# A two-layer decoder trunk on one core: softmax placed behind its own scores, layer 1's memory attentions in one exponential phase, head transposes behind the next projection

## The chip, the cores and the metric

The kernel runs on one core of a Trainium2 chip. The metric is the time of one execution on the device in microseconds (us); less is better. The time of a kernel is the median of several runs. The core's engines work side by side, each through its own instructions in order: TensorE (PE, with its weight loads shown as PEld), VectorE (DVE), ScalarE (ACT), GpSimd (POOL) and SyncE (SP), which issues most DMAs. A semaphore wait at the head of an engine's queue holds everything behind it.

## The reference

512 tokens of width 1024 go through two layers. Layer 1 is a gated DeltaNet with 6 heads of 128, layer 2 a sliding-window attention with 12 heads of 64 and a sink per head. In both, four more heads of 64 attend to 256 fixed memory tokens. Each layer ends with an output projection and a gated feed-forward stage of width 2816.

```python
for layer in range(DEPTH):
    h = rms_norm(x, ln_mix[layer])
    mkv = mem_n @ w_mem_kv[layer]                       # memory keys and values
    if layer < N_A_LAYERS:
        mix_out, mem_q = gated_deltanet_mixer(h, ...)   # q, k, v = silu(conv(h @ w_in)), chunked scan
    else:
        proj = h @ swa_w_q[bl]
        q = apply_partial_rope(proj[..., :SWA_Q_W], cos, sin)
        mix_out = sliding_window_attention(q, shared_k, shared_v, swa_sinks[bl])
        mem_q = proj[..., SWA_Q_W:]
    mem_o = memory_attention(mem_q, mem_k, mem_v)       # softmax(q k / 8) v
    x = x + concatenate([mix_out, mem_o]) @ w_out[layer]
    x = x + swiglu(rms_norm(x, ln_ffn[layer]), w_gate_up[layer], w_down[layer])
return rms_norm(x, ln_final)
```

The softmax of the sliding window takes the sink into the maximum and into the denominator; that of the memories has neither sink nor mask.

## The kernel before

Activations lie transposed, features on the 128 partitions and the 512 tokens along a row. A matrix product in full precision is done as three products of parts (`mm3`, L206): each fp32 operand is split into a rounded high part and a remainder, so a projection of 128 output features is 8 × 3 matmuls of 128x512 into one PSUM bank (`pj`). Its weights come by a DMA (`wraw`, L187), are copied on ACT into the high part (`whi`, L148) and subtracted on DVE into the low part (`wlo`, L161); three pairs of these parts are kept, so weights are prepared ahead.

In layer 1 (`gdn`, L471) the order in the source is: key heads (projection, convolution of four taps as one ACT copy and three DVE steps, SiLU, four transposes on PE, L490 to L503); the decay matrices; gates; the inverses of 32x32 triangular blocks (`base_inverse`, L630: 31 pairs of small DVE steps on `big` and `btmp`, then DMAs); for each of two memory pairs an attention followed by three query heads; the solve of the triangular systems; value heads and the scan over 4 chunks of 128 tokens, for heads 0 to 2 and then 3 to 5 (`scan_step`, L695); the finish of the heads. In layer 2 (`swa`, L1077) a loop over six pairs of heads calls the projection and rotation of the next query pair, the scores of this pair, and `weigh` of the pair before, which holds softmax, transposes of the probabilities (`pt`, copied to `pf`) and the product with the values.

A scheduler of the framework gives each engine its order: the place in the source is a priority, and an instruction is put in line when what it reads is ready by the scheduler's own reckoning. On top of that, functions that need ACT's tables are kept together by hand: `use` (L130) puts a table load ahead, and `fn` (L140) binds each function to it; exponentials and logarithms need one table set, SiLU another. Each switch is an ACT_TABLE_LOAD. In layer 2 the transposes of a pair are bound behind the last score product given out before them.

PSUM has eight banks. Layer 1 uses three for `pj`, two for `g` (transposes, sums, half of the memories' scores) and three for `sc` (scan, other half of the scores, products with the values). Layer 2 uses two for `pj`, one for `g`, two for `qk` (one half of a pair's scores at a time), two for `pt` and one for `sc`. The scores of the window are masked and their maximum is taken by one DVE instruction per block (L752), which writes them to `sm` in SBUF and so frees the `qk` banks; the memories' exponentials in layer 1 read the PSUM banks directly (L142).

Of the kernel before, what the change touches and what calls it, by code (L numbers as in the profile page):

```python
# [18 lines left out]
P = 128  # L19
T = 512  # L20
D = 1024
KD = D // P
H = 6
NC = 4
# [4 lines left out]
EPS = 1e-6  # L29
# [6 lines left out]
LN_EXP = "natural_log_exp_and_others"  # L36
SILU_SIN = "silu_and_others"
# [51 lines left out]
class Builder:  # L89
# [381 lines left out]
    def gdn(self, gp):  # L471
        nc, a, tc = self.nc, self.a, self.tc
# [12 lines left out]
        kn, kg = [], []  # L485
# [22 lines left out]
        f = self.t(gp, [P, 3, NH], F32, "f")  # L508
# [10 lines left out]
        for h in range(H):  # L519
# [4 lines left out]
            ps = self.bank("g")  # L524
# [9 lines left out]
        qg = self.gcr  # L534
# [4 lines left out]
        z, mq, qm, q2 = [], [], [], []  # L539
# [7 lines left out]
        for m in range(2):  # L547
            mq.append(self.pair(self.mpool, f"mq{m}"))
            qm.append(self.t(self.mpool, [P, T], F32, f"qm{m}"))
            self.copy(qm[m], self.normed(4 * H + m))  # L550
        X, Tt = self.base_inverse(gp, base_in)
# [4 lines left out]
        def memory(m):  # L556
            self.use(LN_EXP)
            self.attention(gp, qm[m], self.memK[m], self.memV, m, mq[m])


        for h0 in (0, 3):
            memory(h0 // 3)
            ts = [self.conv_tile(h, self.t(gp, [P, T], F32, "qv", 5)) for h in range(h0, h0 + 3)]
            self.use(SILU_SIN)
            for h, t in zip(range(h0, h0 + 3), ts):
                self.fn(t, t, AF.Silu)
                ps = self.bank("g")
                for c in range(NC):
                    self.mm(ps[:, chunk(c)], kn[h][:, chunk(c)], t[:, chunk(c)])
                self.tt(nc.vector, DT[h], c4(ps), DT[h], ALU.mult)  # L570
                self.tt(nc.vector, qg[h], qg[h], c4(t), ALU.mult)
                sq = self.t(gp, [P, T], F32, "sq", 1)
                nc.scalar.activation(sq, t, AF.Square, scale=math.sqrt(EPS) * P)
                q2.append(self.t(self.dpool, [P, T], F32, f"q2{h}"))
                nc.sync.dma_start(q2[h], sq)
        AT = DT
        vt = []

        def values(heads):
            for h in heads:  # L580
# [8 lines left out]

        S = [None] * H  # L590

        def scan(heads):
            for c in range(NC):
# [127 lines left out]
        return new  # L721


    def attention(self, pool, q, kk, vv, m, out, sinks=None):
        self.weigh(pool, self.scores(pool, q, kk, sinks is not None), vv, m, out, sinks)

    def scores(self, pool, q, kk, win):

        nc = self.nc
        own = "pt" in self.pbufs  # L730
        half = [slice(0, 64), slice(64, P)]
        sm = [self.t(pool, [P, 2, 2, 2 * P], F32, "sm", 4 if own else 2) for _ in range(2)]
        sm = [t[:, n] for t in sm for n in range(2)]
        stats = self.t(pool, [P, 4, 2 * NC], F32, "stats", 2)
        mx, den, nm, es = (stats[:, i, :] for i in range(4))
        for n0 in range(0, NC, 2):
            if own:
# [23 lines left out]
                                accum_out=den[:, i:i + 1])  # L761
        return sm, mx, den, nm, es

    def weigh(self, pool, scores, vv, m, out, sinks):

        nc = self.nc
        win = sinks is not None
        own = "pt" in self.pbufs
        half = [slice(0, 64), slice(64, P)]
        sm, mx, den, nm, es = scores  # L770
        if win:
            sk = sinks.unsqueeze(2).to_broadcast([P, 2, NC])
# [10 lines left out]
                            accum_out=den[:, i:i + 1])  # L783
            self.tt(nc.vector, den, den, es, ALU.add)
        nc.vector.reciprocal(den, den)
        o = self.bank("sc")
        group = NC if own else 2
        for n in range(NC):
            if n % group == 0:
                pf = {}  # L790
            k0 = 1 if win and n == 0 else 0
            p = sm[n][:, :, k0 * P:]
            dn = den.rearrange("p (b n) -> p n b", b=2)[:, n, :]
            for b in range(2):
                if n % 2:
                    self.copy(p[:, b], p[:, b], scale=dn[:, b:b + 1])
                else:
                    self.ts(p[:, b], p[:, b], dn[:, b:b + 1], ALU.mult)
            pt = self.bank("pt" if own else "g", [P, 2, 2, P])
            for j in range(k0, 2):  # L800
                for b in range(2):
# [275 lines left out]
    def swa(self, sp):  # L1077
# [32 lines left out]
        def transpose_values():  # L1110
            v = vv.pop()
            pt = self.bank("g")
            for c in range(NC):
                self.tr(pt[:, c * P:(c + 1) * P], v[:, c * P:(c + 1) * P])
            vt = self.t(sp, [P, NC, P], F32, "vt")
            self.copy(vt.rearrange("p c i -> p (c i)"), pt)
            vv.extend(vt[:, c, :] for c in range(NC))

        def score(t):
            got[t] = self.scores(sp, qs[t], kk[0] if t < 6 else memK[t - 6], t < 6)  # L1120

        def weigh(t):
            mix[t] = self.pair(self.bpool)
            if t < 6:
                self.weigh(sp, got[t], vv, t, mix[t], sinks[:, t, :])
            else:
                self.weigh(sp, got[t], memV, t - 6, mix[t], None)

        got = {}
        queries(6)  # L1130
# [1 line left out]
        keys()  # L1132
        values()
        score(6)
        transpose_values()
        queries(0)
        score(7)
        weigh(6)
        last = 7
# [96 lines left out]
```

## Time and profile before

| | before |
|---|---|
| runs | 1160.89, 1162.48, 1162.56 us |
| median | 1162.48 us |
| profiled execution | 1162.59 us |
| span of its trace | 1160.8 us |
| granted TensorE clock | 0.998 |
| instructions | 19674 |
| PE idle in the span | 25.1 us |
| table loads (L133) | 13, 1.28 us each |

The profile shows one execution. The span is the time from the first to the last instruction; 1.8 us of the execution lie around it. A line of the timeline gives the start, the duration, engine, source line and operation, the tiles written and read, their shape, and in brackets how long the engine was idle before and what it waited for. Matmuls are pipelined, so the recorded time of one is longer than its share of PE's time. Layer 1's mixer ends at about 290 us; the feed-forward stages fill 335 to 655 and 831 to 1150 us; layer 2's attention is between 676 and 776 us.

### The profile page before, as it was taken

The numbers are of one execution on the slowest core, as the hardware profiler recorded it, in microseconds if no ns is written. First come the engines' busy times: TensorE is split into PE (matmuls) and PEld (weight loads), VectorE is DVE, ScalarE is ACT, GpSimd is POOL, SyncE is SP. The second block draws the span as 40 slices with busy tenths as digits, with TensorE's granted clock in tenths as the row PEclk, the third lists the DMA queues.
The fourth block names the chain that finished last, engine by engine and source line by source line (L and its number), as shares of the span: only waits on it lengthen the run. The fifth ranks groups of instructions, "written<-read, shape, count | busy, mean of one in ns | idle before, by whom it ended". The sixth has DMA issues, their size and how long they took to land.

```text
span 1160.8 us, 19674 instructions
## 1 busy us (share of the span) xinstructions
PE 1135.7 (98%) x7476; PEld 995.0 (86%) x7476; DVE 843.1 (73%) x1587; ACT 635.5 (55%) x1273; POOL 85.8 (7%) x97
## 2 busy tenths in 40 slices
PE   7999999999999999999999999999999999999996
PEld 6878777877899998899998777677899988999986
DVE  5754877767789987489866767758799843798754
ACT  7569563366556652256653547675566622566533
POOL 0210000000111100011100000010011100111000
PEclk9999999999999999999999999999999999999999
DMA  8433352225567744567723421143477743577232
GB/s 308 129 108 114 115 127 92 73 91 164 163 141 186 188 124 129 151 149 188 173 75 98 136 73 38 55 99 120 113 186 191 175 111 104 150 188 179 74 93 94
DMA packets 73971, 152.83 MB, mean 132 GB/s; under 512 B 17756, under 2 KB 18420, under 8 KB 73876
## 3 DMA queue, kind: packets, MB, share of 16 engines
q1 hardware_dynamic: 62356, 130.59, 35.9%
q0 software_dynamic: 11520, 20.98, 11.5%
q8 instruction: 59, 0.97, 0.4%
q14 instruction: 36, 0.29, 0.1%
HBM read 144.58 MB, written 6.96 MB: 131 GB/s over the span
## 4 chain that ended last, share of the span: by engine, by line
PE 86%; DVE 8%; ACT 2%; DMA 2%; issue 1%; SPq 0%; DVEq 0%; ACTq 0%
PE pj L154 40%; PE g L154 38%; PE sc L154 6%; DVE wlo L161 2%; PE pt L158 1%; DMA wraw<-in_wout 1%; PE g L158 1%; ACT sm L142 1%; DVE l L164 1%; ACT whi L148 1%; DMA wraw<-in_wmk 1%; DVE btmp L161 1%; DVE big L161 0%; DVE sm L752 0%; PE qk L154 0%
## 5 line engine op out<-in xcount | busy, mean ns | idle before, releaser
L148 ACT ACTIVATE whi<-wraw 128x512 fp32r<-128x512 f32 (+2 forms) x331 | 244.2, 745 | 271.9 <-PE pj L154 175.2
L161 DVE TENSOR_TENSOR wlo<-wraw,whi 128x512 fp32r<-128x512 f32 (+2 forms) x331 | 274.3, 838 | 108.6 <-ACT whi L148 102.7
L154 PE MATMUL pj<-h,whi 128*128 128x512 f32 (+1 forms) x676 | 266.4, 395 | 0.8 <-ACT h L148 0.5
L154 PE MATMUL pj<-l,whi 128*128 128x512 f32 (+1 forms) x676 | 265.2, 392 | 1.2 <-DVE l L164 1.2
L154 PE MATMUL pj<-h,wlo 128*128 128x512 f32 (+1 forms) x676 | 265.3, 393 | 0.0
L154 PE MATMUL g<-T,whi 128*128 128x256 f32 x1280 | 230.3, 282 | 0.0
L154 PEld LDWEIGHTS g<-T,whi 128*128 128x128 f32 x1280 | 197.6, 190 | 1.6 <-DVE fu L164 1.6
L154 PE MATMUL g<-T,wlo 128*128 128x256 f32 x640 | 180.1, 281 | 0.0
L154 PEld LDWEIGHTS pj<-h,whi 128*128 128x128 f32 x676 | 127.1, 188 | 29.7 <-issue 3.0
L154 PEld LDWEIGHTS pj<-l,whi 128*128 128x128 f32 x676 | 127.2, 188 | 28.4 <-DVE l L164 2.0
L154 PEld LDWEIGHTS pj<-h,wlo 128*128 128x128 f32 x676 | 127.3, 188 | 26.3 <-issue 1.9
L154 PE MATMUL g<-h,wlo 128*128 128x256 f32 (+1 forms) x508 | 146.2, 288 | 0.0
L154 PE MATMUL g<-l,whi 128*128 128x256 f32 (+1 forms) x508 | 146.1, 288 | 0.0
L154 PE MATMUL g<-h,whi 128*128 128x256 f32 (+1 forms) x508 | 146.0, 287 | 0.0
L154 PEld LDWEIGHTS g<-T,wlo 128*128 128x128 f32 x640 | 120.2, 188 | 0.0
L154 PEld LDWEIGHTS g<-l,whi 128*128 128x128 f32 x508 | 97.5, 192 | 1.2
L154 PEld LDWEIGHTS g<-h,whi 128*128 128x128 f32 x508 | 95.4, 188 | 1.2
L154 PEld LDWEIGHTS g<-h,wlo 128*128 128x128 f32 x508 | 95.4, 188 | 1.2 <-issue 0.2
L985 POOL DMA_DIRECT2D ws<-in_wgu x40 | 35.2, 879 | 722.9 <-ACT sq L151 246.2
L148 ACT ACTIVATE whi<-ws 128x512 fp32r<-128x512 f32 x80 | 50.4, 631 | 51.2 <-PE g L154 42.0
L161 DVE TENSOR_TENSOR fu<-pj,rstd 128x512 f32<-128x512 f32 (+1 forms) x34 | 22.4, 659 | 54.8 <-PE pj L154 54.8
L161 DVE TENSOR_TENSOR wlo<-ws,whi 128x512 fp32r<-128x512 f32 x80 | 54.8, 685 | 6.9 <-ACT whi L148 6.8
(345 smaller groups left out, 1633.0 us busy)
## 6 DMA issues: line engine op xcount, KB each, us to landing
wraw<-in_wgu SPq DMA_DIRECT2D x48, 512.0 KB, 4.1
ws<-in_wgu SPq DMA_DIRECT2D x80, 256.0 KB, 3.5
ws<-in_wgu POOLq DMA_DIRECT2D x80, 256.0 KB, 4.8
wraw<-in_wdn SPq DMA_DIRECT2D x48, 384.0 KB, 3.2
wraw<-in_win SPq DMA_DIRECT2D x26, 512.0 KB, 3.7
wraw<-in_wgu SPq DMA_DIRECT2D x40, 256.0 KB, 4.4
wraw<-in_wout SPq DMA_DIRECT2D x16, 512.0 KB, 3.6
wraw<-in_wdn SPq DMA_DIRECT2D x16, 256.0 KB, 2.7
```

Of the source, the lines that this page charges most:

```text
L142: ins = self.nc.scalar.activation(out, in_, func, **kw).ins
L148: self.copied = self.nc.scalar.activation(out, in_, AF.Copy, **kw).ins
L154: return self.nc.tensor.matmul(out, lhsT, rhs, start=start, stop=stop, skip_group_check=more).ins
L158: return self.nc.tensor.transpose(out, in_, self.ident[:k, :k]).ins
L161: return eng.tensor_tensor(out=out, in0=a, in1=b, op=op).ins
L164: self.nc.vector.scalar_tensor_tensor(out=out, in0=in0, scalar=scalar, in1=in1, op0=op0, op1=op1)
L985: nc.gpsimd.dma_start(s1, a22, accum_op=ALU.add)
```

## The change

Only the order of calls in the source changes; the same instructions are given out but for two table loads.

- Keys and values: the projection, convolution and SiLU of head h+1 are given out ahead of the transposes of head h.
- `attention` is taken apart into `scores`, `soften` (the softmax) and `weigh` (transposes and products).
- Memories of layer 1: scores and softmax of the first go ahead of the base inverses, those of the second between the second and third query's projection; all six SiLUs come behind in one phase. Two switches of tables go.
- Scan: the last chunk of the first three heads comes behind the values of the second three.
- Layer 2: softmax right behind the products of the pair before, an iteration's part earlier; six `sm` buffers instead of four, three of `stats` instead of two.

```diff
-        for h in range(H):
+        def key(h):
             k = self.conv_tile(H + h, self.t(gp, [P, T], F32, f"kn{h}"))
             self.fn(k, k, AF.Silu)
             kn.append(k)
+        key(0)
+        for h in range(H):
+            if h < H - 1:
+                key(h + 1)
+            k = kn[h]
             ps = self.bank("g")
...
+        def remember(m):
+            got = self.scores(gp, qm[m], self.memK[m], False)
+            self.soften(gp, got, None)
+            return got
+        self.use(LN_EXP)
+        got = remember(0)
         X, Tt = self.base_inverse(gp, base_in)
...
-        for h0 in (0, 3):
-            memory(h0 // 3)
-            ts = [self.conv_tile(h, self.t(gp, [P, T], F32, "qv", 5)) for h in range(h0, h0 + 3)]
-            self.use(SILU_SIN)
-            for h, t in zip(range(h0, h0 + 3), ts):
-                self.fn(t, t, AF.Silu)
...
+        ts = [query(0)]
+        self.weigh(gp, got, self.memV, 0, mq[0], False)
+        ts.append(query(1))
+        got = remember(1)
+        ts.append(query(2))
+        self.weigh(gp, got, self.memV, 1, mq[1], False)
+        self.use(SILU_SIN)
+        for h in range(H):
+            if h + 3 < H:
+                ts.append(query(h + 3))
+            t = ts[h]
+            self.fn(t, t, AF.Silu)
...
         def values(heads):
+            value(heads[0])
             for h in heads:
-                v = self.conv_tile(2 * H + h, self.t(gp, [P, T], F32, "qv", 5))
-                self.fn(v, v, AF.Silu)
+                if h + 1 in heads:
+                    value(h + 1)
+                v = vs[h]
...
         values(first)
-        scan(first)
+        scan(first, range(NC - 1))
         values(second)
+        scan(first, range(NC - 1, NC))
         self.use(LN_EXP)
         scan(second)
...
-        sm = [self.t(pool, [P, 2, 2, 2 * P], F32, "sm", 4 if own else 2) for _ in range(2)]
+        sm = [self.t(pool, [P, 2, 2, 2 * P], F32, "sm", 6 if own else 2) for _ in range(2)]
-        stats = self.t(pool, [P, 4, 2 * NC], F32, "stats", 2)
+        stats = self.t(pool, [P, 4, 2 * NC], F32, "stats", 3 if own else 2)
...
         for t in range(6):
             if t < 5:
                 queries(t + 1)
             score(t)
             weigh(last)
+            soften(t)
             last = t
         weigh(last)
```

What the scheduler makes of it, at three places. First PE at the transposes of key head 1, with the projection of the next key (`pj`) around them; before, and then after:

```order
L154 MATMUL pj_683<-h_479,wlo_680 128x512
L154 MATMUL pj_683<-h_484,whi_679 128x512
L154 MATMUL pj_683<-l_485,whi_679 128x512
L154 MATMUL pj_683<-h_484,wlo_680 128x512
L158 MATMUL g_661<-consts_66,kn_130_624 128x128 x4
L154 MATMUL pj_683<-h_489,whi_679 128x512
```

```order
L154 MATMUL pj_668<-h_484,wlo_665 128x512
L154 MATMUL pj_668<-h_489,whi_664 128x512
L154 MATMUL pj_668<-l_490,whi_664 128x512
L154 MATMUL pj_668<-h_489,wlo_665 128x512
L158 MATMUL g_698<-consts_66,kn_124_609 128x128 x4
L154 MATMUL pj_720<-h_454,whi_716 128x512
```

The transposes have moved behind the last three matmuls of that projection: 14 stood between them and those of key head 0, now 17.

Second ACT at the first memory of layer 1, behind its eight exponentials (`sm` from `g` and `sc`); `qv` is the first query:

```order
L142 ACTIVATE sm_1411,stats_1412<-sc_1428,stats_1412 128x256 x2
L133 ACT_TABLE_LOAD
L148 ACTIVATE sm_1410<-sm_1410,stats_1412 128x256 x2
L148 ACTIVATE sm_1411<-sm_1411,stats_1412 128x256
L148 ACTIVATE pf_1450<-g_1445 128x512
L148 ACTIVATE pf_1459<-g_1454 128x512
L148 ACTIVATE sm_1411<-sm_1411,stats_1412 128x256
L148 ACTIVATE qv_1497<-pj_1504,gains_67 128x512
```

```order
L142 ACTIVATE sm_1273,stats_1274<-sc_1290,stats_1274 128x256 x2
L148 ACTIVATE sm_1272<-sm_1272,stats_1274 128x256 x2
L148 ACTIVATE sm_1273<-sm_1273,stats_1274 128x256 x2
L148 ACTIVATE qv_1450<-pj_1457,gains_67 128x512
L148 ACTIVATE pf_1492<-g_1487 128x512
L148 ACTIVATE pf_1499<-g_1494 128x512
```

The table load is gone, and the fourth scaling and the copy of the query have moved ahead of the two `pf` copies.

Third DVE in an iteration of layer 2, at the reciprocal of the pair before; "ISA" rows at L752 (L774 after) are the masked maxima with the row that stores each one, `q` the next query's rotation, `wlo` a weight split. Before, all four maxima of the first half of scores stand ahead of the rows shown, and the last row is the first maximum of the second half; after, the first ISA row is the first maximum of the first half and the last one the second:

```order
L161 TENSOR_TENSOR stats_7305<-stats_7305 128x8
L161 TENSOR_TENSOR wlo_7925<-wraw_7922,whi_7924 128x1024
L785 RECIPROCAL stats_7305<-stats_7305 128x8
L168 TENSOR_SCALAR sm_7303<-sm_7303,stats_7305 128x128 x2
L168 TENSOR_SCALAR sm_7304<-sm_7304,stats_7305 128x256
L752 ISA sm_7429,stats_7430<-qk_7440,consts_66 128x256
```

```order
L161 TENSOR_TENSOR stats_7325<-stats_7325 128x8
L774 ISA sm_7448,stats_7450<-qk_7451,consts_66 128x128
L774 ISA stats_7450 128x1
L805 RECIPROCAL stats_7325<-stats_7325 128x8
L161 TENSOR_TENSOR q_7442<-q_7442,rs_7443 128x512
L168 TENSOR_SCALAR sm_7323<-sm_7323,stats_7325 128x128 x2
L168 TENSOR_SCALAR sm_7324<-sm_7324,stats_7325 128x256 x2
L774 ISA sm_7448,stats_7450<-qk_7451,consts_66 128x256
```

The reciprocal and the four scalings of the pair before have moved from behind the weight split to ahead of three of the four maxima of this pair's first half. On PE, 14 projection matmuls stood between the two halves of the same pair's scores, and now there are 18.

More of the change, by code (lines that the diff above doesn't have):

```diff
@@ L550, in gdn @@
             self.copy(qm[m], self.normed(4 * H + m))
+        query = lambda h: self.conv_tile(h, self.t(gp, [P, T], F32, "qv", 5))
+        def remember(m):
[4 more added lines that the diff above has]
+        got = remember(0)
         X, Tt = self.base_inverse(gp, base_in)
@@ L554, in gdn @@
             self.copy(kg[h][:, c, :], kg[h][:, c, :], scale=f[:, 2, i:i + 1])
-        def memory(m):
-            self.use(LN_EXP)
-            self.attention(gp, qm[m], self.memK[m], self.memV, m, mq[m])
-        for h0 in (0, 3):
-            memory(h0 // 3)
-            ts = [self.conv_tile(h, self.t(gp, [P, T], F32, "qv", 5)) for h in range(h0, h0 + 3)]
-            self.use(SILU_SIN)
-            for h, t in zip(range(h0, h0 + 3), ts):
-                self.fn(t, t, AF.Silu)
[L567 to L575, printed above, removed]
+        ts = [query(0)]
[10 more added lines that the diff above has]
+            self.fn(t, t, AF.Silu)
+            ps = self.bank("g")
+            for c in range(NC):
+                self.mm(ps[:, chunk(c)], kn[h][:, chunk(c)], t[:, chunk(c)])
+            self.tt(nc.vector, DT[h], c4(ps), DT[h], ALU.mult)
+            self.tt(nc.vector, qg[h], qg[h], c4(t), ALU.mult)
+            sq = self.t(gp, [P, T], F32, "sq", 1)
+            nc.scalar.activation(sq, t, AF.Square, scale=math.sqrt(EPS) * P)
+            q2.append(self.t(self.dpool, [P, T], F32, f"q2{h}"))
+            nc.sync.dma_start(q2[h], sq)
         AT = DT
@@ L590, in gdn, with scan @@
         S = [None] * H
-        def scan(heads):
-            for c in range(NC):
+        def scan(heads, chunks=range(NC)):
+            for c in chunks:
                 for h in heads:
@@ L721, in scan_step @@
         return new
-    def attention(self, pool, q, kk, vv, m, out, sinks=None):
-        self.weigh(pool, self.scores(pool, q, kk, sinks is not None), vv, m, out, sinks)
     def scores(self, pool, q, kk, win):
@@ L762, in scores, with soften @@
         return sm, mx, den, nm, es
-    def weigh(self, pool, scores, vv, m, out, sinks):
+    def soften(self, pool, scores, sinks):
         nc = self.nc
         win = sinks is not None
-        own = "pt" in self.pbufs
-        half = [slice(0, 64), slice(64, P)]
         sm, mx, den, nm, es = scores
@@ L785, in weigh @@
         nc.vector.reciprocal(den, den)
-        o = self.bank("sc")
-        group = NC if own else 2
         for n in range(NC):
-            if n % group == 0:
-                pf = {}
             k0 = 1 if win and n == 0 else 0
@@ L798, in weigh @@
                     self.ts(p[:, b], p[:, b], dn[:, b:b + 1], ALU.mult)
+    def weigh(self, pool, scores, vv, m, out, win):
+        nc = self.nc
+        own = "pt" in self.pbufs
+        half = [slice(0, 64), slice(64, P)]
+        sm = scores[0]
+        o = self.bank("sc")
+        group = NC if own else 2
+        for n in range(NC):
+            if n % group == 0:
+                pf = {}
+            k0 = 1 if win and n == 0 else 0
             pt = self.bank("pt" if own else "g", [P, 2, 2, P])
@@ L1138, in swa @@
         weigh(6)
+        soften(7)
         last = 7
```

11 lines of the change are left out of this document (9 added, 2 removed).

## The prediction

> **What bounds the kernel now.** First I read the page: busy times, and the chain of work that ended last.
>
> ```profile
> PE 1135.7 (98%) x7476; PEld 995.0 (86%) x7476; DVE 843.1 (73%) x1587; ACT 635.5 (55%) x1273; POOL 85.8 (7%) x97
> ...
> PE 86%; DVE 8%; ACT 2%; DMA 2%; issue 1%; SPq 0%; DVEq 0%; ACTq 0%
> ```
>
> TensorE is the bound: busy 1135.7 us, 98% of the span, so about 25 us idle in the whole program, and 86% of the chain that ended last. No matmul or transpose goes and none is added, so the change can only fill or make gaps between PE instructions. The second view is the table of windows over the four stretches in which it moves anything: keys, memories and queries of layer 1, scan, attention of layer 2.
>
> ```profile
> 55.00:100.00 45.00, 44.18 (x215) 36.17 (x214) 22.92 (x33) 35.18 (x104) 8.52 (x6) 1.00 0.34 115
> 120.00:185.00 65.00, 63.21 (x402) 50.42 (x401) 54.70 (x123) 41.75 (x81) 0.00 (x0) 1.00 0.39 112
> 209.00:282.00 73.00, 71.52 (x402) 57.94 (x402) 49.41 (x91) 41.60 (x90) 0.00 (x0) 1.00 0.32 98
> 676.00:776.00 100.00, 97.10 (x688) 72.38 (x687) 68.35 (x230) 68.13 (x207) 0.86 (x1) 1.00 0.18 55
> ```
>
> The columns are the stretch, its length, then busy time and count of PE, PEld, DVE, ACT and POOL, the clock, the DMA share and GB/s. PE is idle 0.8, 1.8, 1.5 and 2.9 us there, 7.0 in all. That understates the gaps a little: the end of a pipelined matmul is modelled and covers part of what follows. So the third view, the timeline of PE, is read from start to start: a projection matmul follows the last one after 0.23 us when nothing holds it, and what is above that is a gap. No DVE or ACT total is near its window (54.7 of 65 at most), so only latencies decide: which tile is late when PE comes to it.
>
> **Keys.** The timeline of PE, then of ACT, at the transposes of key head 1:
>
> ```profile
> 60.38 0.39 PE L154 MATMUL pj<-h,wlo 128*128 128x512 f32 x1
> 61.59 0.66 PE L158 MATMUL g<-consts,kn 128*128 128x128 f32 x4 [0.82 <-ACT kn L142]
> ...
> 60.91 0.63 ACT L142 ACTIVATE kn<-kn 128x512 f32<-128x512 f32 x1 [1.39 <-DVE kn L164]
> ```
>
> PE goes 1.21 us from start to start, 0.98 above the 0.23 of a matmul, because the SiLU ends at 61.54. The new order has three more matmuls of the next projection ahead of these transposes (17 after the last key's transposes instead of 14): 3 × 0.23 = 0.7 us of the gap is filled with work that now follows it, and 0.3 stays. The other heads have no such gap, and moving their transposes gives nothing. Term: **−0.7 us** (from −1.0, all of it, to 0, if the SiLU comes later too).
>
> **Memories of layer 1.** The timelines of PE, DVE and ACT at the first softmax:
>
> ```profile
> 130.19 1.14 PE L154 MATMUL g<-mk,qm 64*128 64x256 f32 x8
> ...
> 132.12 0.50 PE L154 MATMUL pj<-h,whi 128*128 128x512 f32 x1
> ...
> 137.28 0.39 PE L154 MATMUL pj<-l,whi 128*128 128x512 f32 x1
> 139.40 0.30 PE L158 MATMUL g<-consts,sm 128*128 128x128 f32 x1 [1.73 <-DVE sm L168]
> ...
> 138.46 0.19 DVE L785 RECIPROCAL stats<-stats 128x8 f32<-128x8 f32 x1
> ...
> 138.91 0.34 DVE L168 TENSOR_SCALAR sm<-sm,stats 128x256 f32<-128x256 f32 x1
> ...
> 137.82 0.47 ACT L142 ACTIVATE sm<-sc,stats 128x256 f32<-128x256 f32 x1
> ...
> 138.40 1.28 ACT L133 ACT_TABLE_LOAD   x1
> 139.69 1.31 ACT L148 ACTIVATE sm<-sm,stats 128x256 f32<-128x256 f32 x3
> ```
>
> The gap ahead of 139.40 is 2.12 − 0.23 = 1.9 us. The new order takes the table load of 1.28 us from behind the exponentials, but the first transpose waits for DVE's scaling at 138.91, behind the reciprocal at 138.46, behind the last exponential at 137.82; none of these moves, and the same projections stand ahead. So the gap stays, but for some tenths. What the load frees are ACT's scalings (from 139.69 to 138.5) and the copies behind; the new order spends this at once, since all four scalings and the copy of the first query now stand ahead of the copies of turned probabilities (pf), where before there were three scalings. PE waits for those in its next step: one scaling (0.44) and one copy as long or longer, so I put 0.5 to 0.9 us on that.
>
> Of the second memory the scores stood in three pieces on PE:
>
> ```profile
> 156.71 1.14 PE L154 MATMUL sc<-mk,qm 64*128 64x256 f32 x8
> 157.78 0.50 PE L154 MATMUL pj<-h,whi 128*128 128x512 f32 x1
> ...
> 162.16 1.13 PE L154 MATMUL g<-mk,qm 64*128 64x256 f32 x4
> 163.22 0.50 PE L154 MATMUL pj<-l,whi 128*128 128x512 f32 x1
> 163.65 1.13 PE L154 MATMUL g<-mk,qm 64*128 64x256 f32 x4
> 164.71 0.50 PE L154 MATMUL pj<-h,wlo 128*128 128x512 f32 x1
> ```
>
> They cost 1.07 + 1.06 + 1.06 = 3.2 us; the first memory's, in one piece, cost 132.12 − 130.19 = 1.9. In the new order they are in one piece: −1.3. Against it, ACT's exponentials of this softmax now have the copy of the base inverses between them (big, wider than any other copy there) and its scalings follow a projection sooner: I put gaps of 0.3 to 0.5 us on each of three waits, 1.2 in all. Sum: −0.4 for the first gap, +0.7 for pf, −1.3 for the pieces, +0.7 from the second memory where half of its 1.2 falls on work that PE can pull forward: **−0.3 us**. Bounds: −3.2 if gap and pieces go and nothing new comes, +1.5 if all of both new waits is paid and the first gap stays. The two table loads taken out are 2 × 1.28 = 2.6 us of an ACT that is busy 41.75 of 65 us, so they have no term of their own.
>
> The Trainium skill (ScalarE: Activation LUTs, section "What ACT_TABLE_LOAD costs") gives a switch 2.66 us, 1.28 for the load and 1.38 for a drain. Here the load of 1.28 us starts at 138.40 and ACT's next instruction at 139.69, so no drain shows behind it. By that rule the two loads would give ACT 5.3 us rather than 2.6 and, if PE waited for both in full, a memory term near −3; by the rows it stays at −0.3.
>
> **Scan.** The one large gap stands at the transposes of the last value head:
>
> ```profile
> 247.53 0.66 PE L158 MATMUL g<-consts,qv 128*128 128x128 f32 x4
> ...
> 252.31 0.38 PE L154 MATMUL sc<-DT,vn 128*128 128x128 f32 x2
> 253.58 0.66 PE L158 MATMUL g<-consts,qv 128*128 128x128 f32 x4 [0.89 <-ACT qv L142]
> ```
>
> It is 1.27 us from start to start, about 1.0 of gap, for a SiLU of ACT. From the transposes of the head before (247.53) to the gap PE had 4.8 us of work. Now the first group's last chunk of three heads stands there with projections of the output: 4 transposes (0.4), 14 pairs of 128x128 products at 0.22 and 8 projection matmuls at 0.23, 5.3, and the switches between them, some 5.8 us; most of the gap goes, −0.8. In exchange that chunk no longer hides among projections of values: its steps alternate between PE and DVE, and the second group's end has its three finishing sums in a row with only nine matmuls (2 us) behind the last scan step. I put +0.5 on the two. Term **−0.3 us**, from −1.0 (the gap goes and nothing comes) to +1.5 (it stays, and one and a half of its size comes).
>
> **Layer 2.** The gaps ahead of the transposes, iteration by iteration; the timelines of PE, DVE and ACT:
>
> ```profile
> 726.53 1.13 PE L154 MATMUL qk<-ks,q 64*128 64x256 f32 x8
> 728.20 0.54 PE L158 MATMUL pt<-consts,sm 128*128 128x128 f32 x3 [0.53 <-DVE sm L168]
> ...
> 734.91 0.51 PE L154 MATMUL pj<-h,whi 128*128 128x512 f32 x1
> ...
> 738.29 1.14 PE L154 MATMUL qk<-ks,q 64*128 64x256 f32 x8
> 739.69 1.13 PE L158 MATMUL pt<-consts,sm 128*128 128x128 f32 x6 [0.27 <-DVE sm L168]
> ...
> 749.68 1.14 PE L154 MATMUL qk<-ks,q 64*128 64x256 f32 x8
> 751.39 0.54 PE L158 MATMUL pt<-consts,sm 128*128 128x128 f32 x3 [0.58 <-DVE sm L168]
> ...
> 734.28 0.73 DVE L1072 STREAM_SHUFFLE rs<-pj 128x512 f32<-128x512 f32 x1
> ...
> 737.89 1.22 DVE L161 TENSOR_TENSOR wlo<-wraw,whi 128x1024 fp32r<-128x1024 f32 x1
> 739.02 0.20 DVE L785 RECIPROCAL stats<-stats 128x8 f32<-128x8 f32 x1
> 739.26 1.01 DVE L168 TENSOR_SCALAR sm<-sm,stats 128x128 f32<-128x128 f32 x4
> ...
> 735.00 0.50 ACT L142 ACTIVATE sm<-sm,stats 128x256 f32<-128x256 f32 x1
> ...
> 739.32 1.31 ACT L148 ACTIVATE sm<-sm,stats 128x256 f32<-128x256 f32 x3 [2.77 <-DVE stats L785]
> ```
>
> A second half of scores (qk) takes about 1.07 us of PE when nothing follows late; here the transposes come after 1.67, 1.40 and 1.71, so 0.6 + 0.3 + 0.6 = 1.5 us of gap. The two iterations not shown I put at the smallest of the three, 0.3 each: 2.1 in all. The exponentials end by 735.4, yet the reciprocal runs at 739.02: DVE had it in line behind the next query's rotation and a weight split of 1.2 us. The change puts the softmax a place earlier in the source, so reciprocal and scalings come ahead of these, and the transposes are ready when PE arrives. Transposes and projections, now cut into pieces of one to three, become whole: by the switches between them an estimated 0.9 us (0.1 for each of nine pieces joined). Gain 3.0.
>
> The new wait: the sum of denominators (0.1), reciprocal (0.2) and four scalings (1.0), 1.3 us together, now stand ahead of three of the four band maxima of the first half of scores. These free the bank that the second half is written to. Before, DVE went from the rotation's start at 734.28 to behind the last maximum, where the weight split starts at 737.89, in 3.6 us, while PE had 14 matmuls from 734.91 to 738.29, just long enough. Now DVE takes 4.9, to 739.2, and PE has 18 matmuls, 0.9 us more, to 739.2: even in that iteration, and the others have 17 to 19. Where the exponentials end later than DVE arrives, or PE is not held before, it waits 0.2 to 0.6 us. Four iterations with about 0.35 and 0.4 for the last: 1.8. Term 1.8 − 3.0 = **−1.2 us**, from −3.0 (no new wait) to +0.5 (0.6 in five iterations, and half of the small gaps stay). The gap of the first iteration, behind exponentials that end late, is not in the sum, since their order on ACT is the same.
>
> **Sum.** −0.7 − 0.3 − 0.3 − 1.2 = −2.5 us. The profiled execution took 1162.59 us, of which the span is 1160.8; it stands 0.1 above the median of 1162.48, so 1160.1 by that execution and **1160.0** as a median. The two feed-forward stages are not touched and stay. The sync queue gets the same transfers, with the base inverses' 10 now in a row ahead of the squares of the queries; the solve that reads them still comes behind all six queries, so nothing is due from them.
>
> **The rivals.** A measurement of this kernel can tell about 0.2% (2.3 us) from no change.
>
> (1) All gaps go: no new waits. Then −1.0 −3.2 −1.0 −3.0 = −8.2: about 1154.3. For it: no engine but PE is near full in any window. Against it: each softmax is a chain of some 9 us on two engines, and PE has 24 matmuls (5.5 us) to lay beside it.
>
> (2) The gaps change places: each new wait eats its gain (pf and the copy of the base inverses in the memories, band maxima in layer 2, the end of the scan). Then only the keys' 0.7 is left: about 1161.9. For it speaks that DVE and ACT have the same work in another order; against it, that reciprocal and scalings stood ready and idle in layer 2.
>
> (3) Slower: in layer 2 DVE's queue is blocked by the reciprocal. It waits there for the last exponential of ACT, and behind it stand the rotation's last add, the band maxima and the weight split that the next projection needs. Before, the exponentials end at 735.4, and DVE would come to the reciprocal at about 736.3, so it has 0.9 us in hand (maxima and adds before it, 2.0 us behind the rotation's start). If ACT, which gets its four scalings (4 × 0.44 = 1.75 us) an iteration's part earlier, ends later than that by 1.2 us in each of five iterations, PE pays 1.2 + 0.35 each, 7.8, against 3.0 won: +4.8, with the other terms +3.5: about 1166. It decides at 0.9 us of delay of the last exponential.
>
> **How the numbers follow.** My forecast has 0.52, all gaps gone 0.17, gaps that change places 0.20, the blocked queue 0.11. The forecast's own bounds run from 1157 to 1162; the range reaches into (1) and (2) and stops short of (3)'s centre: 1155.0 to 1163.6. Faster by over 0.2% means below 1160.15: 0.33 of my 0.52 and all of (1), 0.50. Slower by over 0.2%, over 1164.8, is (3) with 0.11, and 0.39 is left for no change.
>
> **What the profile after should show.** In the keys' stretch, a gap at the second head's transposes of 0.3 us instead of 1.0. In the memories' stretch 11 table loads in all instead of 13, the first transposes still waiting for DVE's scaling by over 1 us, the second memory's scores in one piece, and from the first memory's scores to the first matmul of the solve about as long as before. In layer 2, transposes straight behind the second half of scores with no wait for sm, and in its place a wait of that half for DVE. I am wrong if the second half of scores never waits (then layer 2 gives 3), if the first gap of the memories goes, or if DVE's idle time ahead of its reciprocal appears.

## The result, and the profile after

The changed kernel takes 1159.29 us (median of nine runs, 1156.72 to 1160.46) where the kernel before takes 1162.43 beside it (nine runs, 1159.96 to 1163.83). The ratio is 0.9976, with a 95% interval of 0.9965 to 0.9987: 2.8 us faster, a little over what can be told from no change. The prediction of 1160.0 (1155.0 to 1163.6) held it. Its profiled execution is the fastest of the nine, 1156.72 us with a span of 1155.0, so the two spans must not simply be subtracted. The timeline of PE tells where they part. This table takes, from each trace, the start of the matmul that opens each stage; the last columns are the lengths.

| from | before, start | after, start | length before | length after |
|---|---|---|---|---|
| first matmul to first transposes of keys | 6.92 | 6.79 | 49.99 | 49.62 |
| keys, to first memory scores | 56.91 | 56.41 | 73.28 | 72.19 |
| memories and queries, to solve | 130.19 | 128.60 | 53.91 | 53.49 |
| solve, values, scan, to first 256-column product of feed-forward 1 | 184.10 | 182.09 | 151.01 | 150.48 |
| feed-forward 1, to first scores of layer 2 | 335.11 | 332.57 | 341.51 | 341.50 |
| layer 2, to last product with values | 676.62 | 674.07 | 96.90 | 95.60 |
| output, to first 256-column product of feed-forward 2 | 773.52 | 769.67 | 57.27 | 55.24 |
| feed-forward 2, to last matmul | 830.79 | 824.91 | 321.79 | 321.77 |

The four changed stages give 1.09 + 0.42 + 0.53 + 1.30 = 3.3 us. Eight products of the last query stood in the memories' stretch before and stand in the solve's after, about 1.06 us of work by the kernel with the memories alone below, so those two lengths are best read together. The 2.0 of the output stage lie in a stretch that the change doesn't touch. The timelines of ACT and PE before, and then of ACT after, name it: a weight copy on ACT waits for its DMA, once 5.31 and once 3.10 us, and what stands behind it on ACT comes about 2 us later; PE pays at the end of the stage, where the next projection waits 0.52 and 0.87 us for the normed activations (`h`, `l`) before and 0.1 after.

```profile
786.59 1.06 ACT L148 ACTIVATE whi<-wraw 128x1024 fp32r<-128x1024 f32 x1 [5.31 <-DMA wraw<-in_wout]
...
811.49 0.50 PE L154 MATMUL pj<-h,whi 128*128 128x512 f32 x1 [0.52 <-ACT h L148]
812.86 0.50 PE L154 MATMUL pj<-l,whi 128*128 128x512 f32 x1 [0.87 <-DVE l L164]
```

```profile
780.53 1.06 ACT L148 ACTIVATE whi<-wraw 128x1024 fp32r<-128x1024 f32 x1 [3.10 <-DMA wraw<-in_wout]
```

The experiments below leave 54.8 to 57.6 us in this stage (once 59.1, with 1.7 of half clock in it, see the last section), with layer 2's change and without it, so it is scatter from run to run. The two feed-forward stages, which nothing disturbs, agree to 0.02 us between the traces: so exact is the comparison where nothing waits. Where something does, a single pair of traces can mislead, as the keys' stage will show.

The page after, beside the lines shown before: busy times, chain, and the group of table loads.

```profile
PE 1131.5 (98%) x7476; PEld 992.9 (86%) x7476; DVE 842.6 (73%) x1587; ACT 631.7 (55%) x1271; POOL 86.0 (7%) x97
...
PE 85%; DVE 8%; ACT 3%; DMA 3%; issue 1%; SPq 0%; DVEq 0%; ACTq 0%
...
L133 ACT ACT_TABLE_LOAD x11 | 14.1, 1283 | 0.9 <-PEq L1262 0.7
```

Two table loads are gone, and nothing else in the counts. In the memories' stage the timelines of PE, ACT and DVE show three gaps:

```profile
135.91 0.39 PE L154 MATMUL pj<-h,wlo 128*128 128x512 f32 x1
137.42 1.16 PE L158 MATMUL g<-consts,sm 128*128 128x128 f32 x8 [1.12 <-DVE sm L168]
...
138.65 0.39 PE L154 MATMUL pj<-l,whi 128*128 128x512 f32 x1
139.55 1.14 PE L154 MATMUL sc<-pf,mv 128*64 128x128 f32 x16 [0.51 <-ACT pf L148]
...
158.35 0.39 PE L154 MATMUL pj<-h,whi 128*128 128x512 f32 x1
160.65 0.61 PE L158 MATMUL g<-consts,sm 128*128 128x128 f32 x3 [1.92 <-DVE sm L168]
...
155.20 0.48 ACT L142 ACTIVATE sm<-g,stats 128x256 f32<-128x256 f32 x1
...
155.96 2.12 ACT L148 ACTIVATE big<-big 96x1024 f32<-96x1024 f32 x1 [0.19 <-DVE big L161]
157.97 0.47 ACT L142 ACTIVATE sm<-sc,stats 128x256 f32<-128x256 f32 x1
...
152.04 0.74 DVE L164 SCALAR_TENSOR_TENSOR qv<-pj,gains,qv 128x509 f32<-128x509 f32 x1
...
152.85 0.68 DVE L778 TENSOR_REDUCE stats<-g 128x2 f32<-128x512 f32 x1
...
159.91 0.20 DVE L805 RECIPROCAL stats<-stats 128x8 f32<-128x8 f32 x1 [3.84 <-ACT sm L142]
```

Less the 0.23 of a matmul, the gap at the first transposes is 1.3 (1.9 before), pf costs 0.7, and at the second memory's transposes stands a new gap of 2.1 us: between its exponentials ACT copies the base inverses for 2.12, and DVE's reciprocal idles 3.84 for them.

### The profile page after: what moved, and what is told of

Same layout as the page of the kernel before. It is cut to its first block, busy times and chain, and to the rows that moved or that the text cites. A ratio compares the mean times of both kernels' runs of the same rounds, so it can differ in the third digit from the quotient of the medians.

```text
span 1155.0 us, 19665 instructions
## 1 busy us (share of the span) xinstructions
PE 1131.5 (98%) x7476; PEld 992.9 (86%) x7476; DVE 842.6 (73%) x1587; ACT 631.7 (55%) x1271; POOL 86.0 (7%) x97
## 4 chain that ended last, share of the span: by engine, by line
PE 85%; DVE 8%; ACT 3%; DMA 3%; issue 1%; SPq 0%; DVEq 0%; ACTq 0%
PE pj L154 40%; PE g L154 38%; PE sc L154 5%; DVE wlo L161 2%; ACT sm L142 1%; PE pt L158 1%; DMA wraw<-in_wout 1%; PE qk L154 1%; ACT whi L148 1%; PE g L158 1%; DVE l L164 1%; DMA wraw<-in_wmk 1%; DVE btmp L161 1%; DVE stats L778 1%; DVE big L161 1%
```

## The experiments

A stretch given below is that of the table, from each kernel's own trace. The 1.7 us that a half clock takes in five of these traces (last section) is named where it falls into one. Each ratio is to executions of the kernel before that were taken beside the run, in three groups with medians of 1160.83, 1161.42 and 1161.81 us; so ratios, not times, compare from one experiment to another.

### Each part alone, on the kernel before

Keys alone:

```diff
+        key(0)
         for h in range(H):
+            if h < H - 1:
+                key(h + 1)
+            k = kn[h]
```

> Before with the key heads' part alone (projection, convolution and SiLU of head h+1 ahead of the transposes of head h). Theory 1, the parts are independent and the gap at key head 1 is what goes: from the first key transposes to the first memory scores on PE 72.2 us as in the changed kernel (before 73.3), all later stages as before, total -1.1 us. My prediction's term was -0.7. Rival, the gap reappears later because DVE and ACT have the same work left: the stage gets shorter by under 0.3 or the memories' stage longer by as much.

1160.47 us, ratio 0.9994 (0.9984 to 1.0003). The keys' stage took 72.23, 1.05 less than in the trace before, and the later ones 53.84, 150.98 and 96.85, as before. But in the six traces that have the old order of the keys this stage takes 72.45 to 73.28, 72.9 in the mean, and the trace before has the longest. So the part is worth about 0.6 us by the traces, which the ratio alone can't tell from nothing.

Memories alone (the `remember` and `weigh` calls of the change):

> Before with the memories' part alone (one exponential phase, two table loads fewer). Theory 1, new waits eat the gain: from the first memory scores to the first matmul of the solve 53.5 us (before 53.9), with eight products of the last query (about 0.9 us) moved behind the solve's first matmul, so the whole is between +0.7 and 0. In the trace a gap of about 2 us ahead of the second memory's first transposes, which was not there before. Rival, the removed table loads pay: 2.5 us or more off this stage.

1161.32 us, ratio 1.0006 (0.9996 to 1.0016). The stage took 54.85, of which 1.7 is half clock, so 53.15; the stretch behind it 152.07 with the last query's products in it, 1.06 more. Together +0.3: taking two loads away brings nothing by itself. The new gap of 2.1 us is there. Layer 2 has the source of before here, but the scheduler gave it another order, and it took 96.03 us instead of 96.90; so the ratio is not that of the memories alone.

Values and scan alone:

```diff
-        scan(first)
+        scan(first, range(NC - 1))
         values(second)
+        scan(first, range(NC - 1, NC))
```

with the values' order as in the change.

> Before with the value heads' and scan's part alone (value h+1 ahead of the transposes of head h; the last chunk of the first three heads behind the second values). Theory 1: the gap of 1.0 us at the last value head's transposes goes and nothing as large comes: from the first matmul of the solve to the first feed-forward product of 256 columns 149.4 us or a little more (before 151.0; the changed kernel has 150.5 with 0.9 to 1.1 of query products in it that were ahead before). My prediction's term was -0.3. Rival, the end of the scan pays it back: 150.7 or more.

1158.19 us, ratio 0.9976 (0.9967 to 0.9986): as much as the whole change. The stretch took 148.93, 2.1 less.

Layer 2 alone:

> Before with layer 2's part alone (softmax behind the products of the pair before, six sm and three stats buffers). Theory 1: from the first scores to the last products with values 95.6 us (before 96.9), and the output stage behind it as it falls, since it hangs on when a weight transfer lands (57.3 in the trace before, 55.2 in the changed kernel's). Rival: the output stage is shorter because of this change (DVE comes to it with less work left): 55.2 here too, and in every trace of a kernel with this part, against 57.3 in every trace without it.

1159.51 us, ratio 0.9991 (0.9982 to 1.0001). Layer 2 took 95.65, 1.25 less. The output stage took 56.86, and 55.18 in the kernel with the keys alone, which has the order of before there; the rival falls.

### The change without its memories' part

```diff
-        self.use(LN_EXP)
-        got = remember(0)
         X, Tt = self.base_inverse(gp, base_in)
...
+        for h0 in (0, 3):
+            memory(h0 // 3)
+            ts = [self.conv_tile(h, ...) for h in range(h0, h0 + 3)]
+            self.use(SILU_SIN)
```

> The changed kernel with the memories of layer 1 put back as they were (keys, values, scan and layer 2 stay changed). Theory 1, the memories' part costs more than it brings and the parts add up: faster than the changed kernel by 0.5 to 1 us, that is 1157 to 1158.5 beside a before of 1161 (ratio about 0.9965); from the first matmul of the solve to the first feed-forward product of 256 columns about 149, from the first memory scores to the solve 53.9. Rival: in the whole kernel the memories' part pays, since what follows it starts earlier; then this kernel is slower than the changed one, ratio 0.998 or more.

1156.63 us, ratio 0.9959 (0.9943 to 0.9974) where the whole change has 0.9976 (0.9965 to 0.9987). The intervals overlap, but the stages say the same: 55.73 less 1.7 of half clock, and 148.90, together 202.9, against 204.0 after the change. In company of the others the memories' part costs about 1 us by the stages.

### Values or chunk

With the values' order alone (`value(h + 1)` ahead of the transposes):

> Before with the value heads alone (value h+1 ahead of the transposes of head h, the scan's order as before). The values' and scan's part together took 2.1 us off the stretch from the solve's first matmul to the first feed-forward product of 256 columns (151.0 to 148.9). Theory 1, the gain is the filler that the scan's last chunk makes for the last value head, so it needs the chunk's move: here the gap of 1.0 us at the last value head stays, and the stretch is 150.5 to 151.0. Rival, the values' order does it: 149.5 or less.

1161.0 us, ratio 0.9992 (0.9982 to 1.0001); the stretch 150.84, and the gap is where it was, as the timeline of PE shows:

```profile
251.81 0.38 PE L154 MATMUL sc<-DT,vn 128*128 128x128 f32 x2
253.07 0.66 PE L158 MATMUL g<-consts,qv 128*128 128x128 f32 x4 [0.89 <-ACT qv L142]
```

With the chunk's move alone:

> Before with the move of the scan's last chunk alone (values in their old order). Theory 1: the gap at the last value head and those at the end of the scan (0.4 and 0.55 in the trace before) go: 149.5 or less for the stretch (151.0 before, 148.9 with both parts). Rival: without the values' new order the transposes of the values wait as before, 150.3 or more.

1158.74 us, ratio 0.9975 (0.9965 to 0.9986); the stretch 148.88, all of the 2.1 us. The same transposes come without a wait:

```profile
250.39 0.40 PE L154 MATMUL pj<-mq0h,wlo 128*128 128x512 f32 x1
250.63 0.60 PE L158 MATMUL g<-consts,qv 128*128 128x128 f32 x4
```

Here 1.0 of the 2.1 is this gap. The gaps of 0.3 behind it, of 0.2 in the first scan and of 0.55 at the scan's end are not in this trace either. So the chunk's move does it: it is work of PE to lay behind the last projection, and the values' order is worth nothing here.

### The table loads put back

The changed kernel with its two loads restored:

```diff
         got = remember(0)
+        self.use(SILU_SIN)
...
         ts.append(query(1))
+        self.use(LN_EXP)
         got = remember(1)
```

> The changed kernel with the two table loads put back, one behind the first memory's exponentials and one ahead of the second's. Theory 1, as in the prediction's rows: the first transposes wait for DVE's scaling and not for ACT, and the loads stand in ACT's waits; from the first memory scores to the solve at most 1.0 us more than the 53.5 of the changed kernel, through the scalings and pf copies that stand behind the first load. Rival, each switch is on the path in full: 2.6 us more by the 1.28 us of a load's row, 5.3 by the Trainium skill's 2.66 us for a switch.

1159.07 us, ratio 0.998 (0.997 to 0.9991): no different from the changed kernel. The stage took 54.84 with 1.7 of half clock in it, 53.1 without, not more than the 53.5 of the change. The timelines of ACT and PE show how a load of 1.28 us costs nothing:

```profile
137.08 1.28 ACT L133 ACT_TABLE_LOAD   x1
138.37 1.71 ACT L148 ACTIVATE sm<-sm,stats 128x256 f32<-128x256 f32 x4
...
138.01 0.72 PE L158 MATMUL g<-consts,sm 128*128 128x128 f32 x4 [0.95 <-DVE sm L168]
138.93 0.84 PE L158 MATMUL g<-consts,sm 128*128 128x128 f32 x3 [0.21 <-ACT sm L148]
```

The first transposes wait for DVE all the same, and ACT's later scalings then hold PE for 0.2. By the Trainium skill (ScalarE: Activation LUTs, section "What ACT_TABLE_LOAD costs") a switch takes 2.66 us with a drain; here ACT's next instruction starts 0.01 us behind the load's 1.28, and the whole shows neither price.

### The copy off ACT, and the weighing later

The copy of the base inverses on GpSimd:

```diff
-        self.copy(Xt, X.rearrange("p i m -> p m i"))
+        nc.gpsimd.tensor_copy(Xt, X.rearrange("p i m -> p m i"))
```

> The changed kernel with the copy of the base inverses on GpSimd instead of ACT. Theory 1, the new 2.1 us gap at the second memory's transposes is there because this copy of 2.1 us stands between the exponentials on ACT: the gap goes to 0.2 or less and the stage from the first memory scores to the solve from 53.5 to 51.5. Rival, the gap is there because DVE takes the maxima late (behind the convolution of the second query and the last steps of the inverses): the exponentials close up, but the gap stays over 1 us.

1156.82 us, ratio 0.996 (0.9945 to 0.9975). The stage took 52.41 instead of 53.49, and the gap is halved. The timeline of PE:

```profile
157.74 0.39 PE L154 MATMUL pj<-h,wlo 128*128 128x512 f32 x1
159.10 0.83 PE L158 MATMUL g<-consts,sm 128*128 128x128 f32 x5 [0.97 <-DVE sm L168]
```

Both theories have a half: 0.9 was the copy, and 1.1 stays. By the timeline it stays because DVE takes the maxima late; no run tested this half alone. In the changed kernel's trace the second memory's scores end at 150.0, but the first maximum starts at 152.85, behind the second query's convolution (its last step at 152.04).

The weighing one projection later:

```diff
         ts = [query(0)]
-        self.weigh(gp, got, self.memV, 0, mq[0], False)
         ts.append(query(1))
+        self.weigh(gp, got, self.memV, 0, mq[0], False)
         got = remember(1)
         ts.append(query(2))
+        ts.append(query(3))
         self.weigh(gp, got, self.memV, 1, mq[1], False)
...
-            if h + 3 < H:
-                ts.append(query(h + 3))
+            if h + 4 < H:
+                ts.append(query(h + 4))
```

> The changed kernel with the transposes and products of each memory one query's projection later in the source (behind the second and the fourth query). Theory 1, the chain of a softmax is longer than one projection (some 7 to 11 us against 5.4) and one more projection covers it: no gap over 0.3 us at the transposes of either memory, the stage from the first memory scores to the solve 53.5 - 1.3 - 0.7 - 0.3 - 2.1 = about 49.5 (before 53.9), the whole 1155 to 1156 beside a before of 1161. Rival, the order then puts the work late and the gap turns up at the query products or the solve: 52 or more.

1158.08 us, ratio 0.9974 (0.9964 to 0.9983), no better than the changed kernel. No transposes wait any more, but the stage took 51.87, not 49.5, though eight more products of queries have moved out of it into the stretch behind (151.32, 0.8 more than after the change): a gap of 3.3 us turned up one step further, at the products with the values of the second memory.

```profile
161.58 0.40 PE L154 MATMUL pj<-h,whi 128*128 128x512 f32 x1
165.15 1.03 PE L154 MATMUL sc<-pf,mv 128*64 128x128 f32 x14 [3.17 <-ACT pf L148]
```

ACT's queue now had the table load, the copy of the inverses and two queries' SiLUs ahead of these pf copies. Neither theory had named this place.

Both edits together:

> The changed kernel with the weighing one query later and the copy of the base inverses on GpSimd. In the kernel with the weighing alone, a gap of 3.3 us turned up at the second memory's products with the values: pf stands on ACT behind the table load, the copy of the inverses (2.1 us) and the first queries' SiLUs. Theory 1, ACT's queue sets it: without the copy the gap is 3.3 - 2.1 = 1.2 us, the stage 51.9 - 2.1 = 49.8 us. Rival, the gap hangs on DVE or PE: it stays over 2.

1156.31 us, ratio 0.9952 (0.9937 to 0.9967). The stage took 52.36 with 1.7 of half clock, 50.7 without, and the stretch behind it 151.94; the gap shrank from 3.3 to 2.3, not to 1.2. ACT was done with the scalings 2.0 us earlier (158.85 against 160.87), but had one more weight copy of 1.0 us in line ahead of pf (163.44 against 164.52).

The same two edits, with the table load bound behind the second memory's last ACT copy, so that pf comes ahead of the SiLUs:

```diff
         self.use(SILU_SIN)
+        self.nosync(self.table_ins, self.copied)
```

> As the one with both, and the SiLU table load bound behind the second memory's last ACT copy, so that the pf copies stand ahead of the queries' SiLUs. Theory 1, ACT's queue: no gap over 0.5 us in the stage from the first memory scores to the solve, 48.7 us, the whole 1154.5 to 1156 (ratio 0.995). Rival, the SiLUs and the squares (each waits for the transfer of the one before) now come too late: gaps of over 1 us at the query products or ahead of the value heads' transposes, and no gain over the one with both.

1154.63 us, ratio 0.9935 (0.9919 to 0.9952): faster than the kernel before and the changed one. The stage took 48.84 (forecast 48.7, before 53.91), of which sixteen products of queries have moved out against the kernel before; the stretch behind it took 151.26, so the late SiLUs cost nothing large. The transposes of the second memory and its products now come like this:

```profile
159.12 1.03 PE L158 MATMUL g<-consts,sm 128*128 128x128 f32 x8
...
161.26 1.15 PE L154 MATMUL sc<-pf,mv 128*64 128x128 f32 x16
```

From the first memory scores to feed-forward 1, where the moved products don't count, the traces give 204.9 us before, 204.0 after the change, 202.9 without the memories' part, 202.4 with the copy on GpSimd, 203.2 with the later weighing, 202.6 with both and 200.1 with the bound load, the half clock's 1.7 taken off where it falls into one.

## Why the prediction was right, and where it was not

The total was right, and so was the frame: no engine's sum decided, only which tile was late. Of the four terms the keys' was right. Layer 2's had the right size from two errors that cancelled, and the memories' and the scan's were wrong and cancelled each other. That the total came so close is in good part luck.

**Keys, −0.7 forecast, about −0.6 measured.** Mechanism and size were right. In this pair of traces the stage gives −1.09, because after the change the SiLU starts 59.97 − 56.41 = 3.56 us behind the first key's transposes, where it was 60.91 − 56.91 = 4.00, so the transposes find it done. The timelines of ACT and PE after:

```profile
59.97 0.63 ACT L142 ACTIVATE kn<-kn 128x512 f32<-128x512 f32 x1 [0.96 <-DVE kn L164]
...
60.55 0.39 PE L154 MATMUL pj<-h,wlo 128*128 128x512 f32 x1
60.78 0.60 PE L158 MATMUL g<-consts,kn 128*128 128x128 f32 x4
```

But the start of this SiLU scatters. In the six traces with the old order of the keys it lies 2.94 to 4.00 us behind those transposes, and the gap at key head 1 is 0 to 0.98; the mean of the stage is 72.9. In the eight with the new order the stage takes 72.19 to 72.56, 72.3 in the mean. In one of them, the kernel with both edits, the SiLU starts at 3.94, and a gap of 0.24 stays, as forecast.

**Memories, −0.3 forecast, +0.3 alone and about +1.0 in company.** That the first gap stays and pf costs 0.5 to 0.9 was right (1.3 and 0.7), and so was that the table loads have no term; putting them back showed it. The step that failed is "gaps of 0.3 to 0.5 us on each of three waits" for the second memory. There was one gap of 2.1 us, and I had the copy of the inverses as one wait among three, without its price, and not the convolution that stands ahead of the maxima on DVE. Moving the copy took 0.9 of it away; a projection more of cover took the gap at the transposes away. The upper bound of +1.5 doesn't follow from its own terms either: 0.9 + 1.2 − 1.3 is 0.8.

**Scan, −0.3 forecast, −2.1 measured alone and −1.6 in company.** The gap at the last value head went, as forecast. The step that failed is "+0.5 on the two" for the chunk that "no longer hides among projections of values": it paid nothing back. The smaller gaps at the scan's end went as well when the chunk alone was moved. In the whole kernel one of these, 0.5, is there again, and the stretch, less the 1.1 of query products moved into it, is at 149.4.

**Layer 2, −1.2 forecast, −1.25 measured, from other terms.** Both were too large. The new wait of 1.8 us for the band maxima is not there: DVE went through its chain in 4.6 us, 730.91 to 735.50, where I had 4.9, and PE came to the second half of scores 0.5 behind its end. The second half never waits longer than before in any iteration, which the prediction gave as a sign of being wrong; but the layer then gave 1.25 us and not 3. The timelines of PE and DVE after:

```profile
735.97 1.13 PE L154 MATMUL qk<-ks,q 64*128 64x256 f32 x8
737.04 1.56 PE L158 MATMUL pt<-consts,sm 128*128 128x128 f32 x10
...
757.66 0.48 PE L154 MATMUL pj<-l,whi 128*128 128x512 f32 x1
758.42 1.14 PE L158 MATMUL pt<-consts,sm 128*128 128x128 f32 x8 [0.28 <-ACT pf L148]
...
730.91 0.73 DVE L1101 STREAM_SHUFFLE rs<-pj 128x512 f32<-128x512 f32 x1
...
735.50 1.22 DVE L161 TENSOR_TENSOR wlo<-wraw,whi 128x1024 fp32r<-128x1024 f32 x1
```

The transposes follow the scores after 1.07 us, with no gap, so the 1.5 us of the three gaps shown did go. The rest of the gain of 3.0 fell short. The 0.6 for iterations not shown was not there to win: no other transposes right behind a second half of scores wait in the trace before. And a wait that I did not have came, 0.5 us for a pf copy at 758.42, in the last iteration. What the joined pieces brought was not measured apart.

Of the rivals, the second (gaps change places) is what happened in the memories, and only there. The blocked queue of layer 2 didn't come; its margin was 0.8 us and not 0.9, since the last exponential shown ends at 735.00 + 0.50 = 735.50.

## What to carry to other kernels

Where the bound engine never waits long, put a price on every instruction that stands between a softmax's steps in a side engine's queue; a copy of 2 us between exponentials costs more than two table loads off the path bring. Work that is ready, such as a scan's chunk, is worth more behind the last projection than among others that have fillers already. And when a gap is covered, look at the next wait of the same chain: here it went from the transposes to the products and left only when the queue's order followed. A gap of 1 us in one trace is not yet its size: at the keys it was between 0 and 1.0 in six traces of the same order.

## What the runs showed of the hardware that was not expected

Inside the program, five of the fourteen traces show the granted clock at a half for 3.41 us, which costs 1.7 us each time. Four of these stretches follow a gap of 2.0 to 2.3 us on PE in the memories' stage, the fifth two gaps of 1.3 and 1.2 in the output stage of the fastest kernel. But the changed kernel's trace has a gap of 2.1 and no such stretch, nor has the one with the gap of 3.3. What parts them can be read from the traces' record of the clock: every half-clock stretch begins a whole number of times 3.413 us (37, 44, 44, 45 and 233 times) behind the start of the full clock. Here are such windows of the kernel with the memories alone, of the changed kernel and of the one with the later weighing, two each around the gap. The number behind the length is PE's busy time, and the clock is the third from the end:

```profile
159.30:162.71 3.41, 1.49 (x11) 1.30 (x11) 2.08 (x7) 3.41 (x12) 0.00 (x0) 1.00 0.92 194
162.72:166.13 3.41, 3.41 (x21) 2.27 (x20) 1.91 (x3) 2.85 (x4) 0.00 (x0) 0.50 1.03 153
...
156.89:160.30 3.41, 1.84 (x9) 1.19 (x7) 0.35 (x2) 3.41 (x10) 0.00 (x0) 1.00 0.77 213
160.30:163.71 3.41, 3.06 (x27) 2.50 (x29) 3.15 (x7) 3.39 (x8) 0.00 (x0) 1.00 0.95 155
...
160.07:163.48 3.41, 1.91 (x13) 1.39 (x11) 1.90 (x3) 3.41 (x8) 0.00 (x0) 1.00 1.00 199
163.48:166.89 3.41, 1.74 (x22) 1.50 (x23) 3.41 (x6) 3.41 (x7) 0.00 (x0) 1.00 1.07 160
```

In the first the gap falls whole into one window, in which PE idles 1.92 us, and the next has half the clock. In the second 1.57 us fall into one window, and in the third the long gap is split into 1.50 and 1.67. All windows of all fourteen traces agree with this, the end of the program included: after 1.79 us or more of idle PE the next window is at half clock, after 1.73 or less it is not. So a gap of 2 us can cost nearly as much again, and whether it does hangs on where it falls among these windows. This was found in the traces afterwards; no run was made to test it.

In the kernel with both edits one of DVE's four scalings took 2195 ns, the others 343 to 354, while GpSimd copied the inverses in 2152 ns (156.34 to 158.49). The fastest kernel shows the same, 2210 ns beside a copy of 2174. In both, the slow scaling starts 0.12 us behind the start of the copy and ends 0.16 us behind its end, so it looks as if it was held for the length of the copy; no run tested it.
